# Key weights for later chunks split in the second chunk, first key products in another order, and an early table load, in a two-layer encoder on one core

## The chip, the cores and the metric

The kernel runs on one core of one Trainium2 chip. The core has five engines with a queue of instructions each: TensorE (PE in the profile; its weight loads are PEld), VectorE (DVE), ScalarE (ACT), GpSimd (POOL) and SyncE (SP), which only issues DMAs. The metric is the device time of one execution in microseconds; less is better. Three runs of the kernel before took 1535.63, 1535.51 and 1534.77 us, a median of 1535.51.

## The reference

A two-layer encoder runs over a prompt of 2048 tokens and, with the same weights, over a sample of 512. D_MODEL is 1024, there are 16 heads of 64 and 4 key/value heads, all in float32. The attention layer, cut to what matters here:

```
def attention_layer(x, g, w_in, w_out, sink, rel_bias):
    b, s, _ = x.shape
    h = rmsnorm(x, g)
    z = h @ w_in
    q = z[..., :ATTN_WIDTH].reshape(b, s, N_HEADS, HEAD_DIM)
    k = z[..., ATTN_WIDTH:ATTN_WIDTH + KV_WIDTH].reshape(b, s, N_KV_HEADS, HEAD_DIM)
    v = z[..., ATTN_WIDTH + KV_WIDTH:ATTN_WIDTH + 2 * KV_WIDTH].reshape(b, s, N_KV_HEADS, HEAD_DIM)
    gate = z[..., ATTN_WIDTH + 2 * KV_WIDTH:]
    o = banded_gqa_with_sink(q, k, v, rel_bias, sink)
    return x + (o * jax.nn.silu(gate)) @ w_out
```

`banded_gqa_with_sink` lets each query block of 128 see three key blocks, with a relative-position bias and a sink logit for each head. A Fourier layer and a last norm follow; the change touches neither.

## The kernel before

The attention layer runs in five chunks of 512 tokens (CHUNKS): chunk 0 is the sample, chunks 1 to 4 are the prompt. Each chunk goes through the same stages. `make_h` loads the transposed input in eight tiles `xk` of 128 channels, multiplies each by the inverse norms (on GpSimd, in chunks 1 to 4, where the tile is 640 tokens wide with a halo of 128), and makes `h` from it. `kv_proj` multiplies `h` with the key weights (the 48 products named K here) and with the value weights. Then 16 + 3 steps interleave the q and gate projections of one pair of heads with scores, softmax and attention of others, in an order written out by hand (PERIOD; FIRST for chunk 0), and the output projection follows, whose second half ends at the start of the next chunk's key products.

Each float32 operand is split into a high part (a cast to fp32r on ScalarE) and a low part (operand less high part, on VectorE or GpSimd). One product is then three matmuls: high by high, high by low, low by high (`matmul3`). `wk_0` and `wk_1` are the two tiles of key weights (w_in tiles 8 and 9), `w32k_0` and `w32k_1` their unsplit float32 (512 KB each), `wv`, `wq`, `wg` and `wo` the others, named alike. In chunk 0 a weight tile is split as it is used, and the split, 1 MB, is stored to DRAM (`wsd`) for the later chunks. Tiles in AGAIN are not stored in chunk 0: chunk 1 loads the unsplit tile, splits it again (cast on ScalarE, subtraction on VectorE) and stores it. Tiles in LATE, the key weights, are loaded a second time by side steps of chunk 0 (`late_w`): cast, subtraction in pieces on GpSimd and store, in steps 2 to 5.

All tiles live in pools with few slots, so an allocation waits for the readers of the tile that had its slot: four slots hold split weights (tag "w"), four hold xk tiles and unsplit weights (tag "x"). Each engine works its queue in program order, and a waiting instruction holds up all behind it. The tiles `xrl` are the last rows of the residual sum of a chunk: VectorE adds the products of the output projection's second half, and GpSimd's queue stores them to `x1d`.

At the start TensorE runs ten warm-up matmuls on constants (L303) and one 8x8 transposition of the norm's gains (L305), from which VectorE makes `g0s`. The key weights of chunk 0 come in five pieces (`piece`), the first of 256 columns on ScalarE's DMA queue, the others on SyncE's.

Of the kernel before, what the change touches and what calls it, by code (L numbers as in the profile page):

```python
# [20 lines left out]
P = 128  # L21
# [8 lines left out]
WARM = 10  # L30
BIG = 2.0 ** 100
LINE = 512
LATE = (8, 9)
AGAIN = (0, 10, 11, 12)
CH = 512
PERIOD = (
# [19 lines left out]
def encoder(  # L56
# [90 lines left out]
    def load_w(c, n, name, lo_engine=None, late=None, w32=None):  # L147

        w = wp.tile([P, 2, D], F32R, align_bytes=LINE, tag="w", bufs=4, name=f"w{name}")
        if c == 1 and n in AGAIN:  # L150
            w32 = xtile([P, D], F32, f"w32{name}")
            SP.dma_start(w32, w_in[n])
            ACT.copy(w[:, 0], w32)
            DVE.tensor_tensor(w[:, 1], w32, f32(w[:, 0]), ALU.subtract)
            POOL.dma_start(f32(wsd[n]), f32(w))
            return w[:, 0], w[:, 1]
        if c:
            SP.dma_start(f32(w), f32(wsd[n]))
            return w[:, 0], w[:, 1]
        if w32 is None:  # L160
            w32 = fetch_w(n, name, late)
        ACT.copy(w[:, 0], w32)
        if lo_engine is None:

            for i in range(4):
                cs = slice(i * 256, i * 256 + 256)
                POOL.tensor_tensor(w[:, 1, cs], w32[:, cs], f32(w[:, 0, cs]), ALU.subtract)
        else:
            last_low[0] = lo_engine.tensor_tensor(w[:, 1], w32, f32(w[:, 0]), ALU.subtract)
        if late or n not in LATE + AGAIN:  # L170
            (SP if lo_engine else POOL).dma_start(f32(wsd[n]), f32(w))
        return w[:, 0], w[:, 1]

    def split_w(c, n, name, w32):

        w = wp.tile([P, 2, D], F32R, align_bytes=LINE, tag="w", bufs=4, name=f"w{name}")
        seq(ACT, ACT.copy(w[:, 0], w32))

        def low():
            for i in range(4):  # L180
                cs = slice(i * 256, i * 256 + 256)
                POOL.tensor_tensor(w[:, 1, cs], w32[:, cs], f32(w[:, 0, cs]), ALU.subtract)
            if n not in LATE + AGAIN:
                POOL.dma_start(f32(wsd[n]), f32(w))

        return (w[:, 0], w[:, 1]), low
# [3 lines left out]
    def after(ins, anchor):  # L190

        if anchor is not None:
            tc.add_manual_dep(ins.ins, anchor.ins.name, ISSUE, reason="issue order")
# [10 lines left out]
    def attention_phase():  # L204

        with ExitStack() as es:
# [110 lines left out]
            wk2 = [(wk, wk32), None]  # L317
            parts = [(0, 0, 256), (0, 256, 512), (0, 512, 1024), (1, 0, 512), (1, 512, 1024)]

            def piece(i):  # L320
                t, c0, c1 = parts[i]
                if wk2[t] is None:
# [6 lines left out]
                load = (SP if i else ACT).dma_start(w32[:, cs], w_in[8 + t, :, cs])  # L329
                if i:  # L330
                    after(load, last_x[0])
                hi = ACT.copy(w[:, 0, cs], w32[:, cs])
                lo = DVE.tensor_tensor(w[:, 1, cs], w32[:, cs], f32(w[:, 0, cs]), ALU.subtract)
                after(hi, last_h[0])
                after(lo, last_h[1] or spread_g)

            piece(0)
# [47 lines left out]
            def kv_proj(c, hs, halo, norms=None, early=None):  # L385
# [42 lines left out]

                kps = [(pj if c else spt)[t][:, :n] for t in range(2)]
                for k in range(KD):  # L430
                    for t in range(2):
                        matmul3(kps[t], wslice(wk, k, t * P, P), cols(hs[k], own0, n), k == 0, k == KD - 1)
                if halo:
                    ps = spt[0][:, :256]
                    for k in range(KD):
# [656 lines left out]
            for c in range(len(CHUNKS)):  # L1092
# [4 lines left out]
                for s in tail:  # L1097
                    s()
                if c == 1:
                    hs, halo = make_h(c, invb)  # L1100
                if c:
                    invb0 = kv_proj(c, hs, halo)
                else:
                    invb0 = kv_proj(c, hs, halo, first_norms, early)
                rowd, sk = bias
# [51 lines left out]
                    if c == len(CHUNKS) - 1 and i in AHEAD:  # L1157
                        AHEAD[i]()

                def late_w(i):  # L1160
                    w32 = fetch_w(LATE[i], f"late{i}", last_exp[0])

                    def split():
                        hi, lo = (xtile([P, D], F32R, f"late{part}{i}") for part in ("hi", "lo"))
                        seq(ACT, ACT.copy(hi, w32))
                        halves = [[t[:, cs] for t in (lo, w32, f32(hi))] for cs in (slice(0, 512), slice(512, 1024))]
                        pieces(*halves[0], ALU.subtract)
                        POOL.dma_start(f32(wsd[LATE[i]][:, 0]), f32(hi))

                        def rest():  # L1170
                            pieces(*halves[1], ALU.subtract)
                            POOL.dma_start(f32(wsd[LATE[i]][:, 1]), f32(lo))

                        return rest

                    return split

                def side(n):
                    if n in (1, 3):
                        side_steps.append(late_w(n // 2))  # L1180
                    if n in (2, 3, 4, 5):
                        rest = side_steps.pop(0)()
                        if rest:
                            side_steps.insert(0, rest)
                    if k_splits:
                        k_lows.append(k_splits.pop(0)())

                side_steps, k_lows = [], []
                low_q, high_q, low_w = [], [], []
                for n in range(19):  # L1190
                    if c == 0:
# [1152 lines left out]
```

## Time and profile before

| | |
|---|---|
| median of three runs | 1535.51 us |
| the profiled execution | 1535.48 us |
| its span in the trace | 1533.7 us |
| TensorE busy | 1520.7 us |
| VectorE, ScalarE, GpSimd busy | 1119.0, 890.3, 453.1 us |
| moved by DMA | 372.71 MB, mean 243 GB/s |
| first key product / end of chunk 0's key products | 5.34 / 18.85 us |
| first scores of chunk 0 | 39.71 us |
| chunk 1: key products | 211.51 to 222.61 us |

A row of the order of time reads: start in us, duration in us, engine, line of the kernel, operation, output<-input by the program's names, shape, count, and in brackets the engine's idle time ahead of it and what ended that. An engine's name with a q is its queue issuing a DMA. Neighbouring instructions of one kind are joined to one row. A matmul's duration is longer than the distance to the next one, since matmuls overlap: distances between starts give the pace. A row of a window has the length of the window, then for PE, PEld, DVE, ACT and POOL the busy time and the count, the granted clock, the DMA engines' busy share and GB/s.

### The profile page before, as it was taken

To read this page: it belongs to the slowest core of one execution; us is meant where nothing else is said; L and a number is where in the kernel's file an instruction comes from. 1 tells how busy PE (TensorE), PEld (TensorE's weight loads), DVE (VectorE), ACT (ScalarE), POOL (GpSimd) and SP (SyncE) were. 2 spreads that over 40 slices of the span, in tenths; PEclk is the share of its full clock that TensorE was granted. 3 is DMA by queue.
4 is the path that set the end of the run, shared out by engine and by line. 5 is a ranking of instruction groups with operands and counts; after the bars stand their busy time and mean duration, and the time that the engine had idled before them with its cause. 6 is when DMAs were issued, how large, how long until landed. Compare 5 with 4: busy or idle time off the path is not lost.

```text
span 1533.7 us, 33665 instructions
## 1 busy us (share of the span) xinstructions
PE 1520.7 (99%) x13150; PEld 1351.5 (88%) x13150; DVE 1119.0 (73%) x2431; ACT 890.3 (58%) x1925; POOL 453.1 (30%) x616
## 2 busy tenths in 40 slices
PE   9999999999999999999999999999999999999998
PEld 7999889999899998999988899888888888888886
DVE  5898665777538775468764577667888878888896
ACT  6788534787237883268862577646655654243343
POOL 2576652422414323315124142222212111011100
PEclk9999999999999999999999999999999999999999
DMA  8687687785857766867649666584667679557852
GB/s 310 230 308 250 231 337 279 218 304 172 317 202 239 248 215 239 300 212 228 226 169 380 226 211 234 208 298 165 238 207 250 210 247 413 169 180 277 298 184 91
DMA packets 100730, 372.71 MB, mean 243 GB/s; under 512 B 11235, under 2 KB 22251, under 8 KB 83420
## 3 DMA queue, kind: packets, MB, share of 16 engines
q1 hardware_dynamic: 82716, 297.38, 56.1%
q0 software_dynamic: 16688, 70.04, 11.8%
q10 hardware_dynamic: 1168, 3.15, 0.6%
q8 instruction: 103, 1.69, 0.4%
q14 instruction: 55, 0.45, 0.1%
HBM read 280.06 MB, written 90.47 MB: 242 GB/s over the span
## 4 chain that ended last, share of the span: by engine, by line
PE 88%; DVE 7%; issue 2%; ACT 2%; DMA 1%; POOL 0%; POOLq 0%; DVEq 0%; SPq 0%; ACTq 0%
PE pj L524 27%; PE W L134 6%; PE pj L134 6%; PE av L780 6%; PE tp L134 5%; PE spt L661 5%; PE av L134 5%; PE spt L134 4%; PE tp L720 3%; PE Wo L134 3%; PE Z L134 3%; PE fo L134 2%; PE z L1425 2%; PE Zo L134 2%; PE X L134 2%
## 5 line engine op out<-in xcount | busy, mean ns | idle before, releaser
L524 PE MATMUL pj<-h,wg 64*128 64x512 f32 x1920 | 437.7, 388 | 0.0
L524 PE MATMUL pj<-h,wq 64*128 64x512 f32 x1560 | 379.0, 389 | 0.0
L524 PEld LDWEIGHTS pj<-h,wg 64*128 64x128 f32 x1920 | 332.1, 184 | 13.1
L524 PEld LDWEIGHTS pj<-h,wq 64*128 64x128 f32 x1560 | 284.4, 184 | 9.3 <-DVE q L580 0.2
L680 DVE CUSTOM_DVE_ANT_0 S<-spt,b 128x385 f32<-128x385 f32 (+1 forms) x320 | 164.8, 524 | 80.0 <-PE spt L661 77.2
L688 ACT ACTIVATE S<-S 128x385 f32<-128x385 f32 (+1 forms) x320 | 189.2, 592 | 54.9 <-DVE S L680 35.5
L733 ACT CAST pts<-tp 128x768 fp32r<-128x768 f32 (+1 forms) x160 | 121.3, 758 | 77.3 <-PE av L780 43.0
L737 DVE TENSOR_TENSOR pts<-tp,pts 128x768 fp32r<-128x768 f32 (+1 forms) x160 | 144.0, 900 | 11.9 <-ACT pts L733 11.4
L825 POOL TENSOR_TENSOR uT<-o,uT 128x256 fp32r<-128x256 f32 x75 | 56.4, 752 | 228.2 <-ACT uT L821 227.9
L780 PE MATMUL av<-pts,v 64*128 64x256 f32 (+3 forms) x1680 | 122.2, 262 | 1.0 <-DVE pts L737 0.9
L661 PE MATMUL spt<-kwin,qab 64*128 64x384 f32 (+1 forms) x960 | 121.9, 340 | 0.9 <-DVE S L680 0.7
L134 PE MATMUL fo<-wo,tTu 128*128 128x512 f32 x480 | 113.7, 392 | 0.0
L780 PEld LDWEIGHTS av<-pts,v 64*128 64x128 f32 (+1 forms) x1680 | 108.3, 159 | 3.4 <-DVE pts L737 1.6
L134 PEld LDWEIGHTS fo<-wo,tTu 128*128 128x128 f32 x480 | 88.7, 188 | 18.0
L720 PEld LDWEIGHTS tp<-ident,S 64*128 64x128 f32 x1792 | 90.4, 138 | 8.0 <-DVE pts L737 2.6
L720 PE MATMUL tp<-ident,S 64*128 64x64 f32 x1792 | 93.3, 223 | 0.1
L816 POOL TENSOR_TENSOR o<-o,s 128x256 f32<-128x256 f32 x75 | 55.7, 743 | 109.6 <-DVE o L810 86.2
L661 PEld LDWEIGHTS spt<-kwin,qab 64*128 64x128 f32 x960 | 83.7, 187 | 3.7 <-issue 1.8
L703 DVE TENSOR_SCALAR S<-S 128x384 f32<-128x384 f32 (+1 forms) x192 | 84.4, 468 | 0.3
L279 DVE SCALAR_TENSOR_TENSOR h<-xk,g0s,h 128x512 fp32r<-128x512 f32 x40 | 46.9, 1185 | 51.1 <-ACT h L278 51.1
L524 PE MATMUL pj<-wo,uT 64*128 64x512 f32 x360 | 74.7, 390 | 0.0
L278 ACT ACTIVATE h<-xk,g0s 128x512 fp32r<-128x512 f32 x40 | 28.7, 724 | 77.1 <-POOL xk L274 76.3
(379 smaller groups left out, 3360.2 us busy)
## 6 DMA issues: line engine op xcount, KB each, us to landing
wo<-wsd SPq DMA_DIRECT2D x32, 1024.0 KB, 6.4
wq<-wsd SPq DMA_DIRECT2D x31, 1024.0 KB, 6.6
wg<-wsd SPq DMA_DIRECT2D x31, 1024.0 KB, 5.9
x<-x1d SPq DMA_DIRECT2D x40, 512.0 KB, 4.0
b<-b21d SPq DMA_DIRECT2D x40, 512.0 KB, 5.1
b<-rowd SPq DMA_DIRECT2D x40, 384.0 KB, 4.1
xs<-in_x_dram SPq DMA_DIRECT2D x23, 512.0 KB, 6.1
s2d<-gt POOLq DMA_DIRECT2D x40, 256.0 KB, 4.0
```

What stands on the lines that cost most here:

```text
L134: ins = pe(PE.matmul(out, a[i], b[j], start=start and i + j == 0, stop=stop and i == 1, skip_group_check=more))
L524: out.last[h] = pe(PE.matmul(out.ps, a[i], b[j], **out.flags()))
L661: pe(PE.matmul(spt[j][:, 2 + k0 * P : 2 + k1 * P], res["q"][rows, qp, b * P : (b + 1) * P], kwin[g][rows, kp, b * P + k0 * P : b * P + k1 ...
L680: seq(DVE, DVE.tensor_tensor_reduce(out=s[:, e0:e1], in0=ps[:, 1 + e0 : 1 + e1], in1=st["bias"][:, j, 386 - e1 : 386 - e0][:, ::-1], scale ...
L688: last_exp[0] = seq(ACT, ACT.activation(s[:, e0:e1], s[:, e0:e1], AF.Exp, bias=s[:, 386:387], scale=-1.0, accum_out=s[:, 387:388]))
L703: seq(DVE, DVE.tensor_scalar(s[:, ks], s[:, ks], den, None, ALU.mult))
L720: pe(PE.transpose(ps[h][:, kb, j, :], s[rows, j, 1 + kb * P : 1 + (kb + 1) * P], ident[rows, rows]))
L733: seq(ACT, ACT.copy(hi, ps))
L737: seq(DVE, DVE.tensor_tensor(lo, ps, f32(hi), ALU.subtract))
L780: last[i][h] = pe(PE.matmul(to, v, pt, start=not swap and n == 0, stop=swap and n == len(todo[h]) - 1, skip_group_check=True,))
L816: eng.tensor_tensor(o, o, s, ALU.mult)
L825: low = eng.tensor_tensor(lo, o, f32(hi), ALU.subtract)
```

## The change

Four things change.

1. LATE and its side steps are gone. The key weights (8 and 9) are in AGAIN, so chunk 1 loads them unsplit, splits them and stores them. `load_w` for them is called ahead of `make_h` there.
2. The key products of chunk 0 run, for each channel tile k, high by high for both output tiles, then low weight by high h for both, then high weight by low h for both; before, one output tile had its three and then the other.
3. ScalarE begins with a copy of one column of constants (`first`), ahead of which stands the table load, and its DMA of the first weight piece comes behind that.
4. The first piece's high part is cast on VectorE, not on ScalarE.

```
-LATE = (8, 9)
-AGAIN = (0, 10, 11, 12)
+AGAIN = (0, 8, 9, 10, 11, 12)
...
-        if late or n not in LATE + AGAIN:
+        if late or n not in AGAIN:
             (SP if lo_engine else POOL).dma_start(f32(wsd[n]), f32(w))
...
+            ACT.copy(ap.tile([P, 1], F32, tag="first", name="first"), idle[:, :1])
+
             def piece(i):
...
-                hi = ACT.copy(w[:, 0, cs], w32[:, cs])
+                if i:
+                    hi = ACT.copy(w[:, 0, cs], w32[:, cs])
+                    after(hi, last_h[0])
+                else:
+                    after(DVE.tensor_copy(w[:, 0, cs], w32[:, cs]), spread_g)
                 lo = DVE.tensor_tensor(w[:, 1, cs], w32[:, cs], f32(w[:, 0, cs]), ALU.subtract)
-                after(hi, last_h[0])
                 after(lo, last_h[1] or spread_g)
...
                 for k in range(KD):
-                    for t in range(2):
-                        matmul3(kps[t], wslice(wk, k, t * P, P), cols(hs[k], own0, n), k == 0, k == KD - 1)
+                    h = cols(hs[k], own0, n)
+                    if c:
+                        for t in range(2):
+                            matmul3(kps[t], wslice(wk, k, t * P, P), h, k == 0, k == KD - 1)
+                        continue
+                    for i, j in ((0, 0), (1, 0), (0, 1)):
+                        for t in range(2):
+                            a = wslice(wk, k, t * P, P)
+                            PE.matmul(kps[t], a[i], h[j], start=k + i + j == 0, stop=k == KD - 1 and j == 1)
...
                 if c == 1:
+                    early = [load_w(c, 8 + t, f"k{c}_{t}") for t in range(2)]
                     hs, halo = make_h(c, invb)
                 if c:
-                    invb0 = kv_proj(c, hs, halo)
+                    invb0 = kv_proj(c, hs, halo, None, early if c == 1 else None)
...
-                def late_w(i):
-                    w32 = fetch_w(LATE[i], f"late{i}", last_exp[0])
...
                 def side(n):
-                    if n in (1, 3):
-                        side_steps.append(late_w(n // 2))
-                    if n in (2, 3, 4, 5):
-                        rest = side_steps.pop(0)()
-                        if rest:
-                            side_steps.insert(0, rest)
                     if k_splits:
                         k_lows.append(k_splits.pop(0)())
```

The scheduler that orders the queues moves more than these lines. ScalarE's queue at the very start, before:

```order
L300 DMA g0r<-in_g_dram 8x128
L329 DMA w32k_0_183<-in_w_in_dram 128x256
L332 ACT_TABLE_LOAD
L332 CAST wk_0_182<-w32k_0_183 128x256
L278 ACTIVATE h_0_189<-xk_0_187,g0s 128x512
```

and now:

```order
L299 DMA g0r<-in_g_dram 8x128
L319 ACT_TABLE_LOAD
L319 CAST first<-const-bfloat16-1.0 128x1
L330 DMA w32k_0_183<-in_w_in_dram 128x256
L277 ACTIVATE h_0_191<-xk_0_189,g0s 128x512
```

The DMA of the first weight piece moved behind the table load, and the cast of that piece left this queue.

ScalarE's queue in chunk 0 between the value products and the first scores (`invb` holds the inverse norms, `b` the bias with the sinks, `kwin` the key windows), before:

```order
L162 CAST wq_1_470<-w32q_1_471 128x1024
L162 CAST wg_0_512<-w32g_0_513 128x1024
L257 COPY invb_391<-pj_73 128x512
L641 COPY b_0_479<-sk 128x2x2
L398 CAST kwin<-kt_0_453 64x512 x2
L474 ACTIVATE v_16_433<-tp,vsc_16_434 128x4x64
L162 CAST wq_2_517<-w32q_2_518 128x1024
```

and now:

```order
L161 CAST wq_1_472<-w32q_1_473 128x1024
L256 COPY invb_393<-pj_73 128x512
L652 COPY b_0_481<-sk 128x2x2
L161 CAST wg_0_514<-w32g_0_515 128x1024
L402 CAST kwin<-kt_0_455 64x512 x2
L485 ACTIVATE v_16_435<-tp,vsc_16_436 128x4x64
L161 CAST wq_2_519<-w32q_2_520 128x1024
```

The cast of the first gate weights moved behind the copies for `invb` and `b` and stands straight ahead of the key windows. VectorE's low part of the same tile moved alike, behind the two evacuations of the keys; in SyncE's queue the load of the tile moved behind that of `b_0`.

GpSimd's queue at the start of chunk 1, before:

```order
L171 DMA wsd_120<-wo_1_4_3088 128x2048
L167 TENSOR_TENSOR wo_1_6_3121<-w32o_1_6_3122,wo_1_6_3121 128x256 x3
L274 TENSOR_TENSOR xk_0_3162<-xk_0_3162,invb_2947 128x640
L171 DMA wsd_121<-wo_1_6_3121 128x2048
L274 TENSOR_TENSOR xk_1_3171<-xk_1_3171,invb_2947 128x640
L274 TENSOR_TENSOR xk_2_3179<-xk_2_3179,invb_2947 128x640
L274 TENSOR_TENSOR xk_3_3187<-xk_3_3187,invb_2947 128x640
L274 TENSOR_TENSOR xk_4_3195<-xk_4_3195,invb_2947 128x640
L274 TENSOR_TENSOR xk_5_3204<-xk_5_3204,invb_2947 128x640
L274 TENSOR_TENSOR xk_6_3212<-xk_6_3212,invb_2947 128x640
L274 TENSOR_TENSOR xk_7_3220<-xk_7_3220,invb_2947 128x640
L930 DMA x1d<-xrl_3002 128x512 x4
```

and now:

```order
L166 TENSOR_TENSOR wo_1_6_3101<-w32o_1_6_3102,wo_1_6_3101 128x256 x3
L154 DMA wsd_102<-wk_0_3142 128x2048
L170 DMA wsd_121<-wo_1_6_3101 128x2048
L154 DMA wsd_103<-wk_1_3148 128x2048
L273 TENSOR_TENSOR xk_0_3154<-xk_0_3154,invb_2927 128x640
L273 TENSOR_TENSOR xk_1_3163<-xk_1_3163,invb_2927 128x640
L273 TENSOR_TENSOR xk_2_3171<-xk_2_3171,invb_2927 128x640
L273 TENSOR_TENSOR xk_3_3179<-xk_3_3179,invb_2927 128x640
L941 DMA x1d<-xrl_2982 128x512 x4
L273 TENSOR_TENSOR xk_4_3187<-xk_4_3187,invb_2927 128x640
L273 TENSOR_TENSOR xk_5_3196<-xk_5_3196,invb_2927 128x640
L273 TENSOR_TENSOR xk_6_3204<-xk_6_3204,invb_2927 128x640
```

Two new stores, of the split key weights, stand ahead of the first multiply of `xk`, and the four stores of `xrl` moved from behind the last multiply to between the fourth and the fifth. On VectorE the low parts of the two key tiles now stand ahead of `h_0`'s low part, and the four additions into `xrl` moved from behind `h_6` to behind `h_1`. On SyncE the loads of the two unsplit tiles stand ahead of all eight `xk` loads; the two loads of stored splits between them are gone.

More of the change, by code (lines that the diff above doesn't have):

```diff
@@ L182, in low @@
                 POOL.tensor_tensor(w[:, 1, cs], w32[:, cs], f32(w[:, 0, cs]), ALU.subtract)
-            if n not in LATE + AGAIN:
+            if n not in AGAIN:
                 POOL.dma_start(f32(wsd[n]), f32(w))
@@ L1158, in extra @@
                         AHEAD[i]()
-                def late_w(i):
-                    w32 = fetch_w(LATE[i], f"late{i}", last_exp[0])
[L1163 to L1176, printed above, removed]
-                def side(n):
-                    if n in (1, 3):
-                        side_steps.append(late_w(n // 2))
-                    if n in (2, 3, 4, 5):
-                        rest = side_steps.pop(0)()
-                        if rest:
-                            side_steps.insert(0, rest)
+                def side(n):
                     if k_splits:
                         k_lows.append(k_splits.pop(0)())
-                side_steps, k_lows = [], []
+                k_lows = []
                 low_q, high_q, low_w = [], [], []
```

## The prediction

> **What bounds the kernel now.** I read the page first, for the bound, then the order of time at the three places that the change touches, then what TensorE waits for there.
>
> ```profile
> span 1533.7 us, 33665 instructions
> PE 1520.7 (99%) x13150; PEld 1351.5 (88%) x13150; DVE 1119.0 (73%) x2431; ACT 890.3 (58%) x1925; POOL 453.1 (30%) x616
> ```
>
> The chain that ended last, by engine:
>
> ```profile
> PE 88%; DVE 7%; issue 2%; ACT 2%; DMA 1%; POOL 0%; POOLq 0%; DVEq 0%; SPq 0%; ACTq 0%
> ```
>
> TensorE is busy for 99% of the span and carries 88% of the chain that ended last. The change takes no matmul away, so it can gain only where TensorE pauses or runs at a slow pace, and it loses wherever a reordered engine lets TensorE wait. The sum is made against the profiled execution: 1535.48 us, a span of 1533.7 and 1.8 around it; the median of the runs, 1535.51, is the same within 0.03. A measurement of this kernel can tell about 0.2%, 3.1 us, from no change.
>
> **Part 1, the first key products.** TensorE's order of time there, then the same group of products cut at three windows (count, shortest/median/longest in ns, first and last start):
>
> ```profile
> 3.41 0.27 PE L305 MATMUL av<-ident,g0r 8*128 8x8 f32 x1
> 3.62 1.89 PE L303 MATMUL pj<-const-bfloat16-1.0 128*128 128x512 bf16 x4
> 5.34 1.58 PE L134 MATMUL spt<-h,wk 128*128 128x512 f32 x2
> 18.85 0.63 PE L356 MATMUL pj<-ohr,rbs 33*16 33x512 f32 x2
> ```
>
> ```profile
> L134 PE MATMUL spt<-h,wk x9: 556/628/792, 6.1 to 9.7; 128*128 128x512 f32 x9
> L134 PE MATMUL spt<-h,wk x7: 628/628/628, 6.7 to 9.3; 128*128 128x512 f32 x7
> L134 PE MATMUL spt<-h,wk x39: 387/389/556, 9.7 to 18.5; 128*128 128x512 f32 x39
> ```
>
> VectorE's low part of the first h, which the second product wants now:
>
> ```profile
> 5.32 0.75 DVE L279 SCALAR_TENSOR_TENSOR h<-xk,g0s,h 128x512 fp32r<-128x512 f32 x1 [0.20 <-ACT h L278]
> ```
>
> Seven products from 6.7 to 9.3 stand 0.43 us apart (2.6 over 6), 39 from 9.7 to 18.5 stand 0.23 apart (8.8 over 38): the pace doubles at about 10, although the page's clock row shows nines from its first slice. The first ten products start between 5.34 and 9.7; nine intervals of 0.43 are 3.85 of these 4.36 us, so 0.5 is pause, most of it ahead of the second product, which starts at 6.1 when that low part is done (6.07), some ahead of the third (6.7). The new order asks for it at the fifth product, 5.3 + 4 x 0.43 = 7.0, so the pauses go. In half a microsecond 1.2 slow products are done sooner, and as many fast ones, 0.23 each, are left out at the end: **-0.3 us**, if the pace turns when it does now.
>
> It may turn earlier. From the end of the last pause (6.7) to the turn (10 to 10.1) it is 3.3 to 3.4 us. With those pauses gone, the last is the one around the 8x8 transposition, over at 3.62: the turn would come at about 7.0, after 4 slow products, and the other 44 take 44 x 0.2266 = 10.0 (the interval of part 4): an end at 17.0 in place of 18.85, **-1.9 us**. The trace has only this one turn, so a rule can't be told from an accident; I take the early turn as likelier.
>
> The Trainium skill ("TensorE: Matmul & The Clock Gate", Part 1) says that the array runs at half rate until one window of 3413 ns was busy, and that the window is free-running. The 3.4 us here agree with its length; a free-running window would put the new turn anywhere between 4.2 and 7.6, and by it the sum would be some 0.5 us lower at best.
>
> ScalarE's DMA of the first weights now stands behind the table load. The load, and a DMA that ScalarE's queue issues late in the kernel:
>
> ```profile
> 1.75 1.28 ACT L332 ACT_TABLE_LOAD   x1 [1.75 <-issue]
> 995.37 0.37 ACT L821 CAST uT<-av 128x256 fp32r<-128x256 f32 x1 [1.42 <-DVE av L816]
> 995.37 0.33 ACTq L1567 DMA_DIRECT2D g1b<-in_g_dram  x1
> ```
>
> There the DMA goes out while ScalarE computes, so I cost this at nothing; were it held until the load's 1.28 us are over, the weights would come 1.3 late and the early turn would be lost.
>
> **Part 2, the first scores of chunk 0.** The gate's load w32g_0 now goes out behind the bias load b_0, and its split stands ahead of the key windows.
>
> SyncE, ScalarE, VectorE and TensorE in order of time:
>
> ```profile
> 25.55 0.38 SPq L629 DMA_DIRECT2D b<-rowd  x1
> ```
>
> ```profile
> 30.51 0.20 ACT L641 COPY b<-sk 128x4 f32<-128x4 f32 x1 [2.59 <-DMA b<-rowd]
> 30.61 1.26 ACT L398 CAST kwin<-kt 64x512 fp32r<-64x512 f32 x2
> 32.26 1.04 ACT L162 CAST wq<-w32q 128x1024 fp32r<-128x1024 f32 x1
> ```
>
> ```profile
> 31.25 1.39 DVE L403 TENSOR_TENSOR kwin<-kt,kwin 64x512 fp32r<-64x512 f32 x2 [1.95 <-ACT kwin L398]
> 37.10 0.69 DVE L580 SCALAR_TENSOR_TENSOR q<-pj,invb 128x512 f32<-128x512 f32 x1 [1.24 <-PE pj L134]
> ```
>
> ```profile
> 39.71 0.50 PE L661 MATMUL spt<-kwin,qab 64*128 64x256 f32 x4
> ```
>
> The load that now follows b_0, w32q_2, had landed by 32.26, where its cast starts. With w32g_0 in that place its cast (1.04) starts at 32.1, not beside the 2.6 us of idle time ahead of 30.51; the window casts follow to 34.4; VectorE's low part of the gate takes about 1.2 from 33.1, the two window lows (1.39) end near 36, four value lows (0.48 each, two short ones) near 37.8. The evacuation of q, which waited 1.24 for TensorE at 37.10, then starts at 37.8: the cover is 1.24 and all of it is used, 0.7 of it over. Scores come at 40.4 in place of 39.71: **+0.7** in all, part 1 included, if the pace turns as now. With the early turn the chain starts earlier too, since b_0 waits for a store of a row that TensorE makes at 18.85; but it then runs among loads that fill the DMA engines, so I let it gain 1.5 of 1.9: scores at 38.9, **-0.8**. Bounds of parts 1 and 2 together: -1.2 (the whole 1.9) to +1.0.
>
> **Part 3, the side work of chunk 0 goes.** Two loads, two casts, eight subtractions and four stores of late key weights leave steps 2 to 5.
>
> GpSimd and VectorE in one of the steps, what TensorE waited for from 50 to 105, and where the first score product of each step starts:
>
> ```profile
> 64.78 1.45 POOL L962 TENSOR_TENSOR latelo<-w32late,latehi 128x256 fp32r<-128x256 f32 x2
> ```
>
> ```profile
> 65.80 1.24 DVE L585 TENSOR_TENSOR qab<-q,qab 128x512 fp32r<-128x512 f32 x1
> ```
>
> ```profile
> PE av L780 <- DVE pts L737: 0.9, 2, 0.5
> ```
>
> ```profile
> 63.17 0.33 PE L661 MATMUL spt<-kwin,qab 64*128 64x256 f32 x1
> 72.08 0.38 PE L661 MATMUL spt<-kwin,qab 64*128 64x256 f32 x1
> 80.33 0.33 PE L661 MATMUL spt<-kwin,qab 64*128 64x256 f32 x1
> 89.42 0.38 PE L661 MATMUL spt<-kwin,qab 64*128 64x256 f32 x1
> 98.01 0.33 PE L661 MATMUL spt<-kwin,qab 64*128 64x256 f32 x1
> ```
>
> Beside GpSimd's subtractions VectorE's qab low takes 1.24, where the evacuation of q at 37.10, of the same size and with nothing beside it, took 0.69; TensorE then waits twice for VectorE, 0.9 in all. The score starts give steps of 8.91, 8.25, 9.09 and 8.59. The two with subtractions and the one behind them are 0.66, 0.84 and 0.34 over the 8.25 of the step without: 1.8. I take **-1.6**, between 0.9 and 1.8; the two slots and the DMA time that come free are worth nothing on a path that TensorE sets.
>
> **Part 4, the start of chunk 1.** Raw key weights (512 KB) replace stored splits (1 MB), and are split there.
>
> GpSimd, VectorE, SyncE (the issues of xk_3 and xk_4) and TensorE in order of time, and a window of ten us (its last two numbers: DMA share, GB/s):
>
> ```profile
> 196.91 1.56 POOL L274 TENSOR_TENSOR xk<-xk,invb 128x640 f32<-128x640 f32 x1
> 207.98 1.56 POOL L274 TENSOR_TENSOR xk<-xk,invb 128x640 f32<-128x640 f32 x1 [5.84 <-DMA xk<-in_xT_dram]
> 213.23 5.13 POOL L274 TENSOR_TENSOR xk<-xk,invb 128x640 f32<-128x640 f32 x3 [1.46 <-DMA xk<-in_xT_dram]
> 220.33 1.14 POOL L930 DMA_DIRECT2D x1d<-xrl  x2 [1.97 <-DVE xrl L929]
> ```
>
> ```profile
> 199.26 3.43 DVE L279 SCALAR_TENSOR_TENSOR h<-xk,g0s,h 128x512 fp32r<-128x512 f32 x1 [8.63 <-ACT h L278]
> 222.68 2.34 DVE L154 TENSOR_TENSOR wv<-w32v,wv 128x1024 fp32r<-128x1024 f32 x2
> ```
>
> ```profile
> 196.98 6.37 SPq L272 DMA_DIRECT2D xk<-in_xT_dram  x2
> ```
>
> ```profile
> 200.63 1.52 PE L134 MATMUL tp<-wo,uT 128*128 128x512 f32 x6
> 211.51 11.26 PE L134 MATMUL pj<-h,wk 128*128 128x512 f32 x48
> 222.61 1.60 PE L134 MATMUL spt<-wk,hl 128*128 128x256 f32 x12
> ```
>
> ```profile
> 200.00:210.00 10.00, 10.00 (x46) 8.29 (x45) 4.81 (x6) 2.46 (x5) 3.70 (x3) 1.00 1.02 425
> ```
>
> The second weight tile needs the slot of wo_1_2, free at 200.63. A cast of 1.04 (as wq's at 32.26) and a low part of 1.2 (half of 2.34) end at 203; GpSimd's store of it stands ahead of the first multiply of x, which so moves from 196.91 to about 203.5. ScalarE's casts and VectorE's low parts of both tiles stand ahead of h_0 there, which the late multiply covers. xk_3 waits for the slot of the second raw tile, so it is issued at 203 where it was at 196.98, in a stretch whose DMA engines are full (1.02); it took 11 us to its multiply at 207.98. Sharing 425 GB/s between the loads and GpSimd's stores I estimate 9 now: it lands at about 212, and its multiply ends near 213.8. VectorE's four additions into x1 now stand ahead of h_2's low part and wait for the end at 211.51; at 0.69 each, two of them before, h_2 is just in time (214.3). Then come the four x1d stores, 2.3 us, which stood behind the last multiply: xk_4 to xk_7 are multiplied from 216.0 at 1.55 each. TensorE wants h_4 at 211.51 + 4 x 1.36 (six matmuls of 0.2266) = 217; its high part comes at 217.5 + 0.7, its low part at 219.6, since VectorE's low parts wait out GpSimd's multiplies (3.43 at 199.26, beside two of them, against the 0.75 at 5.32). Waits of 2.5 at h_4 and 1.7 at h_5; the products end near 226.6 in place of 222.6: +4.0. Without that lockout I get +2.2, with transfers 0.3 us slower or faster +5.0 or +2.6. The other end: from 211.51 to 222.61 it is 11.1 us, of which 48 x 0.2266 = 10.88 is matmul, so no gain beyond 0.2 is to be had. I take **+3.5**, next to the row of 3.43.
>
> The Trainium skill ("SBUF — State Buffer", Who interferes with whom) has VectorE and GpSimd lock a shared port for a whole instruction where VectorE reads two operands from SBUF, which speaks against this change; by it the sum has +4.0 here, without it +2.2.
>
> **Sum:** 1535.48 - 0.8 - 1.6 + 3.5 = **1536.6 us**.
>
> **Rivals.**
> - **Slower: GpSimd's order costs more.** If xk_3 lands after about 213.5, each microsecond goes through the stores to h_4 one to one; from 5.9 us in part 4 on, the kernel is slower by over 0.2%. At 214.2 it is 6.0: 1535.48 - 0.8 - 1.6 + 6.0 = 1539.1. For it: 11 us from issue to use of xk_3 in the full stretch. Against: 1 MB less to read. 0.2.
> - **The start doesn't do what it says**: the pace turns at 10 as before, or the weights come late. 1535.48 + 0.7 - 1.6 + 3.5 = 1538.1. 0.2.
> - **Part 4 is covered**: if xk_3 is there by 208, the stores wait only for the additions behind 211.5, and the last multiply ends at 219.7 against 218.4, ahead of its use. +0.5: 1533.6. Against it: the lockout. 0.15.
>
> **How the numbers follow.** The forecast has 0.45, by itself 1535.0 to 1538.0. The range takes in the rivals but for the tails: 1533.4 to 1539.3. Slower: the first rival and a quarter of the second, 0.25. Faster by 3.1 us needs part 4 covered and the whole early turn: half of the third, 0.08. The rest is 0.67.
>
> **What would show it.** The products of the first keys end near 17.0 (part 1; 18.5 without the turn); scores begin at 38.9 or 40.4 (part 2); steps of chunk 0 are 8.3 all through (part 3); the first x multiply of chunk 1 near 203.5 less what was gained, the x1d stores between the fourth and the fifth, and the 48 products 14 to 16 us long where they were 11.26 (part 4). The sum is wrong if these products stay under 12 us.

## The result and the profile after

| | before | after |
|---|---|---|
| median of 14 runs each | 1534.76 us (1533.84 to 1538.36) | 1538.48 us (1537.59 to 1542.68) |
| the profiled execution, its span | 1535.48, 1533.7 us | 1540.24, 1537.3 us |
| TensorE busy | 1520.7 us | 1520.2 us |

The ratio of the times is 1.0029, with a 95% interval of 1.0022 to 1.0036: the changed kernel is **slower by 0.29%** by that ratio (the medians lie 3.7 us, 0.24%, apart), and inside the predicted range (1533.4 to 1539.3), 1.9 us above the predicted 1536.6. The chances leaned to "within 0.2%"; the measurement says slower. The profiled execution of before stood 0.7 us above its median, that of after 1.8 above its own.

The page of the changed kernel: its span, the engines, and the chain that ended last by engine.

```profile
span 1537.3 us, 33654 instructions
PE 1520.2 (99%) x13150; PEld 1330.8 (87%) x13150; DVE 1118.2 (73%) x2434; ACT 891.0 (58%) x1925; POOL 445.1 (29%) x606
PE 81%; DVE 7%; DMA 5%; issue 3%; ACT 2%; POOL 2%; SPq 0%; POOLq 0%; DVEq 0%; ACTq 0%
```

TensorE's busy time is 0.5 us less, so the 3.6 us of span are 4.1 us more of idle time; what a slower or faster pace does is inside the busy time. The chain's DMA share is 5% where it was 1%, but that alone names no cause: of its 74 us, 19 lie at the start of chunk 1 (a raw key weight and an `xk` tile), 23 in the first 30 us and the rest behind 1150 us. TensorE in order of time at the start and at the first steps of chunk 0:

```profile
3.62 1.04 PE L302 MATMUL pj<-const-bfloat16-1.0 128*128 128x512 bf16 x4
4.70 3.12 PE L443 MATMUL spt<-h,wk 128*128 128x512 f32 x12
8.35 8.46 PE L443 MATMUL spt<-h,wk 128*128 128x512 f32 x36 [0.54 <-ACT h L277]
16.74 0.63 PE L360 MATMUL pj<-ohr,rbs 33*16 33x512 f32 x2
...
37.66 0.50 PE L672 MATMUL spt<-kwin,qab 64*128 64x256 f32 x4
38.38 0.39 PE L672 MATMUL spt<-kwin,qab 64*128 64x256 f32 x2 [0.22 <-DVE qab L596]
...
44.85 0.60 PE L672 MATMUL spt<-kwin,qab 64*128 64x256 f32 x6
...
53.34 0.38 PE L672 MATMUL spt<-kwin,qab 64*128 64x256 f32 x1
...
61.58 0.33 PE L672 MATMUL spt<-kwin,qab 64*128 64x256 f32 x1
```

The last four warm-up matmuls take 1.04 us where they took 1.89: the pace doubled at about 3.6, ahead of every key product, and the products end at 16.74 where it was 18.85. Scores begin at 37.66 (before 39.71). Step 0 is 7.19 long (37.66 to 44.85), and steps 1 and 2 are 8.49 and 8.24. TensorE at the start of chunk 1:

```profile
208.00 3.11 PE L133 MATMUL pj<-h,wk 128*128 128x512 f32 x13
211.50 1.66 PE L133 MATMUL pj<-h,wk 128*128 128x512 f32 x6 [0.39 <-DVE h L278]
213.73 1.43 PE L133 MATMUL pj<-h,wk 128*128 128x512 f32 x5 [0.58 <-DVE h L278]
215.90 0.51 PE L133 MATMUL pj<-h,wk 128*128 128x512 f32 x1 [0.73 <-ACT h L277]
218.74 7.06 PE L133 MATMUL pj<-h,wk 128*128 128x512 f32 x23 [2.33 <-DVE h L278]
225.64 3.04 PE L133 MATMUL spt<-wk,hl 128*128 128x256 f32 x24
```

The 48 products begin 3.51 us earlier than before (208.00 against 211.51) and end 3.03 later (225.64 against 222.61): 17.64 us long in place of 11.10, **+6.5 us**. From start to start against 0.2266 each, the groups lose 0.55, 0.87, 1.04, 2.61 and 1.69; the first four are the bracketed waits and what lies around them. The last, 1.69, is pace, as the products of one window show (count, shortest/median/longest in ns, first and last start):

```profile
L133 PE MATMUL pj<-h,wk x9: 396/628/796, 218.7 to 222.2; 128*128 128x512 f32 x9
```

Seven of these, from 219.33 to 221.89, stand 0.43 apart: after the wait of 2.33 the pace had halved, as at the program's start. The granted clock of two windows (third from the end) says the same:

```profile
215.20:218.61 3.41, 0.51 (x1) 0.19 (x1) 2.78 (x3) 2.39 (x5) 2.93 (x2) 1.00 0.70 248
218.61:222.03 3.42, 3.29 (x8) 2.62 (x9) 3.42 (x7) 1.59 (x4) 1.57 (x1) 0.50 0.45 153
```

GpSimd and VectorE in order of time, which feed these products:

```profile
200.04 0.53 POOL L154 DMA_DIRECT2D wsd<-wk  x1 [3.14 <-DVE wk L153]
200.59 1.58 POOL L273 TENSOR_TENSOR xk<-xk,invb 128x640 f32<-128x640 f32 x1
...
209.32 1.57 POOL L273 TENSOR_TENSOR xk<-xk,invb 128x640 f32<-128x640 f32 x1 [1.74 <-DMA xk<-in_xT_dram]
210.83 2.19 POOL L941 DMA_DIRECT2D x1d<-xrl  x4
213.04 5.09 POOL L273 TENSOR_TENSOR xk<-xk,invb 128x640 f32<-128x640 f32 x3
```

```profile
211.69 2.00 DVE L278 SCALAR_TENSOR_TENSOR h<-xk,g0s,h 128x512 fp32r<-128x512 f32 x1
213.60 1.64 DVE L289 SCALAR_TENSOR_TENSOR hl<-xk,g0s,hl 128x128 fp32r<-128x128 f32 x1
215.88 2.81 DVE L278 SCALAR_TENSOR_TENSOR h<-xk,g0s,h 128x512 fp32r<-128x512 f32 x1 [0.63 <-ACT h L277]
```

The first multiply follows the second weight store, the fourth waits for its tile until 209.3, the `x1d` stores (2.2 us) hold back the fifth, and four of VectorE's low parts take 2.0 to 2.8 us beside the multiplies where the same operation alone takes 0.75.

One more place, far from the change, loses time. GpSimd near 1187, and TensorE's next wait:

```profile
1187.42 0.55 POOL L1470 DMA_DIRECT2D s2d<-gt  x1 [2.56 <-issue]
1187.98 0.57 POOL L127 TENSOR_TENSOR invb<-invb,mhalf 128x1 f32<-128x1 f32 x1
```

```profile
1192.69 0.71 PE L1323 MATMUL trb<-ident,x 64*128 64x64 f32 x16 [0.61 <-DVE x L1314]
```

In the Fourier layer GpSimd stands for 2.56 us ahead of a store of a tile of `gt` to `s2d`, waiting for nothing that the profile shows ("issue"). The norm behind it comes late, and TensorE is 3.10 us behind before ahead of this place and 3.94 behind it.

### The profile page after: what moved, and what is told of

Read it like the earlier page. It is cut to its first block, busy times and chain, and to the rows that moved or that the text cites. A ratio compares the mean times of both kernels' runs of the same rounds, so it can differ in the third digit from the quotient of the medians.

```text
span 1537.3 us, 33654 instructions
## 1 busy us (share of the span) xinstructions
PE 1520.2 (99%) x13150; PEld 1330.8 (87%) x13150; DVE 1118.2 (73%) x2434; ACT 891.0 (58%) x1925; POOL 445.1 (29%) x606
## 3 DMA queue, kind: packets, MB, share of 16 engines
q8 instruction: 103, 1.69, 0.4%
## 4 chain that ended last, share of the span: by engine, by line
PE 81%; DVE 7%; DMA 5%; issue 3%; ACT 2%; POOL 2%; SPq 0%; POOLq 0%; DVEq 0%; ACTq 0%
PE pj L535 28%; PE av L791 5%; PE spt L672 5%; PE pj L133 5%; PE W L133 5%; PE tp L133 4%; PE av L133 4%; PE tp L731 4%; PE Wo L133 3%; PE spt L133 3%; PE Z L133 2%; PE fo L133 2%; PE Zo L133 2%; PE z L1413 2%; PE X L133 1%
```

## The experiments

Two questions were open: how much the start, the side work and chunk 1 are each worth, and what in chunk 1 costs 6.5 us: the order on GpSimd, the stores' DMA traffic, the slow pace, or VectorE held up by GpSimd. Times are medians, and ratios go against runs of the kernel before on the same chip: e1 to e4 against 1534.27, e5 to e8 against 1534.33, e9 to e11 against 1534.58, e12 against 1534.99.

**e1: the new start alone** (items 2 to 4 of the change, put into the kernel before; the second split stays in chunk 0)

```
+            ACT.copy(ap.tile([P, 1], F32, tag="first", name="first"), idle[:, :1])
...
+                    after(DVE.tensor_copy(w[:, 0, cs], w32[:, cs]), spread_g)
...
+                    for i, j in ((0, 0), (1, 0), (0, 1)):
```

> The kernel before with the three edits of the start alone (table load first, first piece cast on VectorE, new order of the first key products); the side steps of chunk 0 stay. Theory A (the moment at which TensorE's pace doubles is set by a window that runs by itself, not by the edits): the first key products end anywhere from 16.7 to 18.5 us, by where the doubling falls in this execution, and the median of the runs is 0.3 to 2 us below before. Theory B (the edits bring the doubling forward): the products end at 16.7 and the time is 2 us below before. Both: chunk 1's 48 key products take 11.1 us as before.

1534.52 us, ratio 1.0002 (0.9993 to 1.0011): no difference. In its profile the pace turned at 6.4, the key products ended at 16.73 and scores began at 37.93, but step 0 was again 7.19 long, with the same 0.22 of wait for `qab`.

**e2: the split in chunk 1 alone** (item 1; the changed kernel with the old start)

```
-            ACT.copy(ap.tile([P, 1], F32, tag="first", name="first"), idle[:, :1])
...
-                    after(DVE.tensor_copy(w[:, 0, cs], w32[:, cs]), spread_g)
```

> The kernel before with the key weights' split moved to chunk 1 and the side steps gone, start as before. Theory A: steps of chunk 0 are 8.25 us throughout, 1.9 us less in all; chunk 1's key products take 17 to 18 us where before they took 11.1; the time is 4 to 5 us above before. Rival C (most of the loss comes from the start or from elsewhere): the key products of chunk 1 take under 14 us, the time is within 1.5 us of before.

1538.5 us, ratio 1.003 (1.0017 to 1.0042): the whole loss is in item 1. Its start, TensorE in order of time:

```profile
5.24 2.81 PE L133 MATMUL spt<-h,wk 128*128 128x512 f32 x7
8.33 9.63 PE L133 MATMUL spt<-h,wk 128*128 128x512 f32 x41 [0.29 <-DVE h L278]
17.89 0.63 PE L355 MATMUL pj<-ohr,rbs 33*16 33x512 f32 x2
```

The old order with the old pauses had its pace from about 6.5 on in this execution and ended at 17.89. At nearly the same turn the new start of e1 ends at 16.73, so items 2 to 4 together are worth 1.1 to 1.2 us there (0.3 of it is the first product's earlier start, 4.94 against 5.24), and 0.8 at the scores (37.93 against 38.76). Step 0 is 6.69 long here and 7.19 in e1, which takes 0.5 of that back: some 0.3 us net.

**e3: the two stores behind the last multiply** of chunk 1; the rest as in the changed kernel

```
-            POOL.dma_start(f32(wsd[n]), f32(w))
+            if n in (8, 9):
+                kept.append((n, w))
...
+                    for n, w in kept:
+                        after(POOL.dma_start(f32(wsd[n]), f32(w)), last_mul[0])
```

> The changed kernel, but the two stores of the split key weights are issued behind chunk 1's last multiply of x; the queue of GpSimd then has no store among the multiplies, and the xrl stores go back behind them too. Theory A (GpSimd's order makes the wait): chunk 1's key products take 11 to 12.5 us and the time is 2 to 4 us below before. Rival D (the raw weights' loads and slots make x late, whatever GpSimd's order): they take 14 us or more and the time stays above before.

1534.22 us, ratio 1.0 (0.9991 to 1.0009), where a time below before was expected. TensorE at the start of chunk 1, then one window of ten us of the changed kernel and of this one:

```profile
208.37 8.86 PE L133 MATMUL pj<-h,wk 128*128 128x512 f32 x37
217.79 2.83 PE L133 MATMUL pj<-h,wk 128*128 128x512 f32 x11 [0.56 <-DVE h L283]
```

```profile
200.00:210.00 10.00, 10.00 (x45) 8.29 (x45) 6.19 (x9) 3.05 (x6) 5.94 (x5) 1.00 1.02 423
```

```profile
200.00:210.00 10.00, 10.00 (x46) 8.29 (x45) 7.20 (x7) 5.15 (x10) 6.60 (x5) 1.00 0.66 242
```

The products are 12.1 us long: **5.5 of the 6.5 us come back** when two DMA instructions move. The scheduler then also puts the `x1d` stores behind the last multiply again, so order and traffic moved together: the DMA engines are full until 210 in the changed kernel and are done before that here (1.02 against 0.66). e4 to e6 try to take these apart.

**e4: only the `x1d` stores and their additions go late**; the weight stores stay early

```
-                for s in tail:
+                for s in tail[:-1] if c == 1 else tail:
...
+                    tail[-1]()
```

> The changed kernel with the four xrl stores alone moved back behind the last multiply; the two stores of key weights still stand ahead of the first. Theory A, if the xrl stores carry most of it: chunk 1's key products take 12 to 14 us, time 0.5 below to 1.5 above before. If the key weights' stores and slots carry it: 15 us or more, time as the changed kernel.

1538.08 us, ratio 1.0022 (1.0012 to 1.0031); products 16.4 us long. Moving these stores returns 1.2 us of the 6.5.

**e5: no early traffic.** e4's edit, and the early stores write 16 columns only; the full ones follow the last multiply, so the 16 columns are written twice

```
+                POOL.dma_start(f32(wsd[n])[:, :, :16], f32(w)[:, :, :16])
```

> As the kernel with the xrl stores moved back (16.4 us for chunk 1's key products), but at the place of the two early stores GpSimd now stores only 16 columns of each half, and the whole tiles go out behind the last multiply of x. GpSimd still waits for the second tile's low part ahead of its first multiply; 2 MB of traffic is gone from that stretch. Theory E (the stores' traffic makes x late): the third and fourth xk land near 203 and 206, the key products take 11 to 13 us. Theory A (GpSimd's order): they take 15 us or more as before the cut.

1537.91 us, ratio 1.0024 (1.0015 to 1.0033); products 16.5 us long although the traffic is gone (DMA share 0.67 from 200 to 210). The order changed too: the scheduler put the second small store behind the third multiply, so the first multiply starts at 197.93 and not, as in e4, behind both stores at 200.51. VectorE, then GpSimd:

```profile
207.95 5.00 DVE L284 SCALAR_TENSOR_TENSOR h<-xk,g0s,h 128x512 fp32r<-128x512 f32 x1 [0.64 <-ACT h L283]
...
214.99 0.74 DVE L284 SCALAR_TENSOR_TENSOR h<-xk,g0s,h 128x512 fp32r<-128x512 f32 x1
```

```profile
207.76 4.63 POOL L279 TENSOR_TENSOR xk<-xk,invb 128x640 f32<-128x640 f32 x3
216.37 3.07 POOL L279 TENSOR_TENSOR xk<-xk,invb 128x640 f32<-128x640 f32 x2 [3.98 <-DMA xk<-in_xT_dram]
```

One low part took 5.00 us: it began 0.2 behind the start of three multiplies without a gap and ended 0.6 behind the last; 0.74 us is its time with nothing beside it. The last two tiles need the slots that low parts free, so GpSimd waited 4 us for them.

**e6: the two stores on ScalarE's DMA queue**, so that GpSimd doesn't wait for the splits

```
+            (ACT if n in (8, 9) else POOL).dma_start(f32(wsd[n]), f32(w))
```

> The changed kernel with the two stores of split key weights on ScalarE's DMA queue, at the same time but out of GpSimd's queue, whose order is then that of the kernel without them. Theory E (traffic): the fourth xk lands at 209 as in the changed kernel and the key products take 14 us or more. Theory A (GpSimd's order): 11 to 13 us.

1539.56 us, ratio 1.0036 (1.0022 to 1.0049); products 19.3 us long. GpSimd:

```profile
204.36 1.56 POOL L273 TENSOR_TENSOR xk<-xk,invb 128x640 f32<-128x640 f32 x1 [4.43 <-issue]
207.28 6.71 POOL L273 TENSOR_TENSOR xk<-xk,invb 128x640 f32<-128x640 f32 x4 [1.37 <-DMA xk<-in_xT_dram]
```

GpSimd no longer waits for a weight, yet its second multiply starts at 204.36, later than the changed kernel's (202.69); its tile landed at 204.2 there and at 202.6 in the changed kernel. So waiting for the splits alone isn't the cause. The run is no clean test of more than that: the second weight store went out at 206.01, not 200.04, since it stood behind a cast of `h` in ScalarE's queue, and two of the `x1d` stores came ahead of the seventh multiply, where GpSimd waited 2.63 us for VectorE's additions.

**e7: the pace kept up.** Fifteen matmuls on constants, whose result nothing uses, stand behind those of the second to fourth channel tile

```
+FILL = {(1, 1): 2, (2, 1): 3, (3, 1): 10}
...
+                                for _ in range(FILL[k, t]):
+                                    PE.matmul(spt[1], idle[:, :P], idle, start=True, stop=True)
```

> The changed kernel with 15 matmuls on constants, as the warm-ups are, put where TensorE waits in chunk 1's key products: 2 behind the second channel tile, 3 behind the third, 10 behind the fourth (3.4 us at full pace, the waits there were 4.8). Their result is used by nothing. Theory F (the slow stretch of 7 products behind the long wait is the clock falling back): no product is 0.43 us from the next, the 48 products take 15.9 us or less where they took 17.6, time 1 to 2 us below the changed kernel. If the slow stretch has another cause: it stays, and the time is the same or more.

1538.87 us, ratio 1.003 (1.0017 to 1.0042); products and fillers 16.7 us long, where 15.9 or less was expected. No product stands at the slow pace, and the granted clock is 1.00 from 208 to 226, which fits idle time as what brings the slow pace; but the ten fillers run from 217.34 to 219.35, while the next channel tile is ready at 218.25, and the time is no better.

**e8: e3 with ten fills of a small tile at GpSimd's start**, to see whether the 2.56 us near 1187 go by the place of an instruction in GpSimd's program

```
+    for _ in range(10):
+        POOL.memset(pad, 0.0)
```

> The kernel with the stores deferred, and ten small memsets at the start of GpSimd's queue, as many instructions as the changed kernel has fewer than before. Theory G (a fetch of GpSimd's code falls into a chain near 1185 us in every kernel with the shorter queue and costs 0.85 us there): the 2.6 us in which GpSimd waits for nothing shown, ahead of its s2d store, is gone or elsewhere, TensorE loses nothing between 1104 and 1267 us, and the time is 0.9 us less than without the memsets. If the position in the queue isn't the cause, that gap stays.

1533.27 us, ratio 0.9995 (0.9986 to 1.0004). The pause, 2.6 us, stands ahead of the same store, so the number of GpSimd's instructions does not place it.

**e9: the multiplies of chunk 1 on VectorE**, the stores as in the changed kernel

```
+                        last_mul[0] = (DVE if c == 1 else POOL).tensor_tensor(xk[:, :n], xk[:, :n], invb[:, :n], ALU.mult)
```

> The changed kernel with chunk 1's eight multiplies of x on VectorE; GpSimd has only its stores there, the stores of key weights and their traffic stay as they are. Theory H (what keeps h late is that VectorE's low parts wait out GpSimd's multiplies, and that these wait in line behind stores): chunk 1's key products take 11 to 14 us, time 3 to 5 us below the changed kernel. Theory E (traffic alone): the fourth xk lands at 209 as before and the products take 15 us or more.

1540.72 us, ratio 1.0041 (1.0027 to 1.0055), the slowest; products 18.2 us long. VectorE:

```profile
205.42 0.83 DVE L273 TENSOR_TENSOR xk<-xk,invb 128x640 f32<-128x640 f32 x1 [2.56 <-DMA xk<-in_xT_dram]
208.77 0.83 DVE L273 TENSOR_TENSOR xk<-xk,invb 128x640 f32<-128x640 f32 x1 [2.52 <-DMA xk<-in_xT_dram]
209.51 0.75 DVE L281 SCALAR_TENSOR_TENSOR h<-xk,g0s,h 128x512 fp32r<-128x512 f32 x1
...
215.18 1.28 DVE L943 TENSOR_TENSOR xrl<-xrl,tp 128x512 f32<-128x512 f32 x2
216.37 1.28 DVE L943 TENSOR_TENSOR xrl<-xrl,av 128x512 f32<-128x512 f32 x2
```

With nothing on GpSimd the low part takes 0.75, so the lockout is gone, and the loss isn't: the tiles still land late, and each wait now holds up VectorE's own queue, low parts and the four additions with it.

**e10: e9 with the stores of e3, and two DMAs of 4 KB to a scratch tensor at GpSimd's start**

```
+    for t in scratch:
+        POOL.dma_start(t, mhalf)
```

> The kernel with deferred stores, with the eight multiplies on VectorE and two tiny stores to a scratch tensor at the start of GpSimd's queue. Both theories: key products 11 to 12 us. With the two stores GpSimd has issued as many DMAs ahead of the place near 1185 us as in the kernel before; if the 2.6 us gap there follows that number, it is gone and the time is 1 to 2.5 us below before; if not, it stays and the time is 0 to 1.5 below.

1536.32 us, ratio 1.0008 (0.9999 to 1.0017); products 15.5 us long. Without late traffic and without the lockout, VectorE's queue is the bound: an `h` low part waits there behind the four additions, and a stretch at the slow pace follows. So taking the multiplies from GpSimd moves the wait to VectorE's queue and doesn't end it.

**e11: e3 with the two small DMAs of e10**

> The kernel with deferred stores and the two tiny stores at the start of GpSimd's queue, nothing else. If the gap of 2.6 us near 1185 follows the number of GpSimd's DMAs (107 ahead of it in every kernel that has it, 109 or 105 in those that have not): it is gone, TensorE loses under 0.2 between 1104 and 1267 us, time 0.7 to 1 us below the kernel with deferred stores alone. If not: it stays, time as there.

1533.09 us, ratio 0.9992 (0.9983 to 1.0001); products 11.45 us long. GpSimd near the place of the 2.56 us, and ScalarE's row that makes the tile of the first of the three stores:

```profile
1177.68 1.63 POOL L1480 DMA_DIRECT2D s2d<-gt  x3 [5.40 <-ACT jkb L1299]
```

```profile
1174.14 0.63 ACT L1477 ACTIVATE gt<-c 128x512 f32<-128x512 f32 x1
```

The last store of the group no longer pauses, and from 1102 to 1266 TensorE gains 0.9 us on e3. The pause isn't gone, though: it stands two stores earlier. The tile of the first of these three was done at 1174.77 and its store went out 2.9 us later, where the stores around it follow their tiles by 0.3; the releaser that the profile names, `jkb`, is a tile that no store reads. Nothing on TensorE's way waits for that store.

**e12: e11 once more**

> The kernel of e11_defer_two once more, since its interval (0.9983 to 1.0001) touches 1. If its gain is real (first scores 1.8 us earlier, side work 1.9 gone, chunk 1's key products about 0.4 us longer than before's, step 0 longer by 0.5): a ratio of 0.9985 to 0.9995 again, key products under 12.2 us, no wait of GpSimd near 1188. If e11 was a lucky draw of the moment at which the pace doubles: a ratio of 0.9995 to 1.0005, that of e3_defer_w.

1534.2 us, ratio 0.9997 (0.9988 to 1.0006); products 11.9 us long, and the pause again ahead of the store that nothing waits for. So a version without the loss was found, and none that is shown to beat the kernel before.

## Why the prediction was right or wrong

The parts, from the two profiled executions:

| part | predicted | measured | from |
|---|---|---|---|
| 1 and 2, up to the first scores | -0.8 | -2.06 | 39.71 to 37.66 |
| step 0 | 0 | +0.50 | 6.69 to 7.19 |
| 3, side work | -1.6 | -1.95 | the rest of -3.51 at 208.00 |
| 4, key products of chunk 1 | +3.5 | +6.54 | 11.10 to 17.64 |
| Fourier layer | 0 | +0.84 | +3.10 to +3.94 |

They add up to 3.9, against 3.6 in the spans; some 0.2 is won back near the end. The other 1.1 of the 4.8 us between these two executions lies outside the span (2.9 us here, 1.8 before).

**Part 1: the direction held, its rule did not.** The rule was that the pace turns 3.4 us after the last pause, so at 7.0. It turned at 3.6 in the changed kernel, and in the twelve experiments between 4.0 and 6.7, whatever the order of the products: e1 6.4, e2 with the old pauses 6.5, e11 4.7 and e12, the same kernel, 6.1. The moment goes by the execution, not by the edit, and the 10.1 of the trace of before was a late one. So the "early turn", for which the part booked -1.9, was no gain of the change: e2, with the old start, has it too, and of the 2.11 us by which the first products end earlier, 0.96 are there without items 2 to 4 (18.85 against e2's 17.89). The new start gives the other 1.1 to 1.2 (e1 against e2), where the part priced its pauses at 0.3: once the pace has doubled, a pause costs its whole length. With the new start the moment of the turn counts for little, since the products then wait for `h` (0.54 in the changed kernel): in the twelve profiles that have it they end between 16.3 and 17.0, with turns from 3.6 to 6.6. That a prediction of 17.0 by the wrong rule came near 16.74 is luck.

The Trainium skill ("TensorE: Matmul & The Clock Gate", Part 1) has the free-running window of 3413 ns, which the prediction weighed and gave the smaller weight. The runs agree with the Trainium skill on the length and on the window's running by itself: thirteen of the fourteen turns lie within 3.1 us of one another, and in the changed kernel the clock fell at 218.6 and returned at 222.0, which is 63 and 64 windows of 3.413 behind 3.6. They don't fit the earliest moment that the prediction worked out from it, 4.2: the turn at 3.6 ends a window in which TensorE stood idle until 0.77. How busy a window must be for the turn stays open.

**The table load** cost nothing, as predicted. In the changed kernel the DMA of the first weights was issued at 1.41, within the load (1.35 to 2.63).

**Part 2: the size was off, and a piece was missed.** The scores gained the whole 2.06; the part let the chain keep 1.5 of 1.9 and lose 0.7 behind the gate's split. The cover of 1.24 us was used up, as forecast: VectorE's evacuation of `q` starts only 0.8 us earlier than before (36.27 against 37.10), behind the split and the window lows. The price shows one place on: the second pair of scores waits 0.22 for `qab`, and step 0 grows by 0.5. Of the 1.1 us of the new start 0.3 is left at step 1, too little to show in e1's interval. This cause of the 0.5 is read from the two profiles; no run moved the split back alone.

**Part 3 held.** Steps 1 to 7 are 8.24 to 8.49 all through (before up to 9.09), and 1.95 us are gained, just above the bounds of 0.9 to 1.8 (by e2 against before it is 1.83); TensorE waits for VectorE nowhere from 45 to 120.

**Part 4: the right chain, too short.** Predicted were a first multiply near 200.0 (203.5 less the 3.5 gained), stores between the fourth and fifth, and products of 14 to 16 us. Found: 200.6, the stores at 210.8, and 17.6 us. Two sizes were off.
- **The waits**, 4.2 by the working (2.5 at `h_4`, 1.7 at `h_5`; 3.5 was taken net) and 5.1 here: 0.55 at `h_2`, which was forecast to be just in time, 0.87 at `h_3`, and 1.04 and 2.61 at `h_4`. The tile `xk_3` landed 1.3 us behind the first product, between the 0.5 of the forecast and the 2.0 of the slower rival. Beside the multiplies four low parts of VectorE took 2.0 to 2.8 us.
- **The pace**, 1.7, was in no sum: a wait that lasts long enough turns the pace back, and the products behind it pay again. The prediction looked for a turn of the pace at the start alone.

The rival "GpSimd's order costs more" had its threshold at 5.9 in this part; in the profiled execution the loss of 6.5 crossed it, through the lockout (VectorE waiting out GpSimd's multiplies) and the pace more than through the tile's landing. What is shown is that the loss comes with item 1 (e2) and that, with the multiplies on GpSimd, taking the two stores out of the stretch gives 11.5 to 12.1 us (e3, e8, e11, e12). Single remedies do not: without late traffic it is 16.5 us (e5), with the stores out of GpSimd's queue 19.3 (e6), without the lockout 18.2 (e9). The rows suggest links of one chain: the stores' 2 MB make tiles land late (DMA engines full to 210), late tiles bunch the multiplies, bunched multiplies stretch a low part (2.8 us here, 5.00 in e5), and the low part frees the slot for the next tile's load. This chain is argued from the rows; since the scheduler moved other instructions in e3, e5, e6 and e9 as well, no run cuts one link alone.

The Trainium skill ("SBUF — State Buffer", Who interferes with whom) has the lock held for one instruction of the engine that came first. The rows agree that VectorE waits beside GpSimd (0.74 against 2.0 and more, and 0.75 in e9 with nothing on GpSimd), but 5.00 us is longer than one multiply (about 1.55) and the low part together: there it waited out three.

**The Fourier layer** was in no part, since the change touches nothing there. Yet the change takes two DMAs out of GpSimd's program (157 to 155), and the pause keeps to the 115th of them: before, that is the second store of its group, for which nothing waits, and now it is the last one, with the norm behind it. The 0.8 us come back in e11 and e12 with two small DMAs on GpSimd, far ahead, and not in e8 with ten instructions that are no DMAs.

**The sum.** By the experiments, at equal turn, the change is -0.3 (start), -1.9 (side work), +6.5 (chunk 1) and +0.8 (Fourier), +5.1, against +3.7 between the medians and 3.4 to 5.5 by the interval. The slow stretch explains the gap if not every execution meets it, and the granted clocks of the runs speak for that. At half clock for 3.41 us it takes 0.0011 of a run's mean clock. Six of the changed kernel's fourteen runs have 0.999, as 27 of 28 runs of before (those beside e1) have; their median is 1538.22, 3.5 us above before, and the sum without the 1.7 of pace is +3.4. Three have 0.997, the profiled one among them; their median is 1540.24, 5.5 above. Whether the stretch lay in chunk 1 in each of these is not shown.

The range held because it took in the slower rival, and in part by luck: the predicted time was short by the waits of part 4, by a loss of 0.8 at a place that no part covers and, in the runs that meet it, by the pace.

## What to carry to other kernels

Before a pace or a stall of the profiled execution is priced, ask whether it is the kernel's or that execution's: here a turn priced at 1.9 us was the chance of one profile, and e2 had it without the new start. A stall may also move with a count that the change alters far away, as the pause at the 115th DMA did. When work moves to a stretch whose DMA engines are full, count its stores first, and issue those that nobody waits for behind the stretch; here two instructions were worth 0.3% of the time. Waits on TensorE that fill more than two microseconds of a window of 3.4 cost more than themselves here, since the products behind them ran at half pace.

## What the runs showed of the hardware

- **The pace doubles at a moment of its own.** In fourteen profiled executions it turned once at 10.1 us and otherwise between 3.6 and 6.7, with no order by kernel.
- **It falls back at the border of a window of its own, too.** Six profiles have a slow stretch in chunk 1's products (the changed kernel, e2, e4, e6, e9, e10). Each begins within 0.2 us of a whole number of 3.413 after the turn at the start (e2: 6.52 + 62 x 3.413 = 218.13, and the first slow product is at 218.13), and lasts one such window. In the window ahead of it TensorE was idle for 2.1 to 3.2 us, worked out from the starts of its matmuls. Where at most 2.0 us of a window were idle (e5 with waits of up to 2.1 that lie across a border, e7, and e9 in the window before its fall), the pace stayed. The Trainium skill ("TensorE: Matmul & The Clock Gate", Part 1) lets the clock fall after a whole idle window; here some two thirds of one were enough.
- **VectorE can wait out several GpSimd instructions**, not only one: 5.00 us for an operation of 0.74, beside three multiplies that follow one another without a gap.
- **GpSimd pauses about 2.6 us ahead of one DMA of its own, waiting for nothing shown, in all fourteen kernels.** In thirteen it is the 115th DMA of GpSimd's program, which goes out 2.9 us behind the end of the `gt` that it stores, where the stores around it need 0.3. In the changed kernel and in e2, e3, e4, e7, e8 and e9 that is the store ahead of the norm, and TensorE loses 0.8 to 1.0 us; in the others it is one that nothing waits for, and the loss doesn't show. In e5, whose two small stores come early, the idle time ahead of the 113th DMA is 3.16 us where before has 0.60, and its 115th goes out on time. What GpSimd does in that time stays open.
